# A one-core encoder layer: norm by scaled rows and transposes, three weight blocks before the second half of the tokens, a half-width triangular inverse, another order at the end, and new stage times

## The chip, the cores and the metric

The kernel runs on one core of one Trainium2 chip. The metric is the device time of one execution in microseconds; before the change the median of three runs is 1065.43 us (1065.08 to 1065.56). A profile comes from one execution more, and times within it are counted from its first instruction.

## The reference

One layer of an encoder, 512 tokens of 1024 channels in float32: a norm, one wide projection `w_in`, two token-mixing branches, a gated merge through `w_out`, a second norm, a SwiGLU feed-forward, and a last norm.

```python
h = rmsnorm(x, mix_norm[l])
p = h @ w_in[l]
rx, ry, qkv, z, ba, gates = jnp.split(p, SPLIT_IDX, axis=-1)
y_rnn = rglru_branch(rx, ry, ...) @ w_rnn_proj[l]        # conv, gates by 128x128 blocks, scans both ways
y_dn = deltanet_branch(qkv, z, ba, ...) @ w_dn_proj[l]   # 8 heads, both ways, a triangular solve per chunk
g_rnn, g_dn = jnp.split(jax.nn.sigmoid(gates), 2, axis=-1)
x = x + (g_rnn * y_rnn + g_dn * y_dn) @ w_out[l]
h = rmsnorm(x, ffn_norm[l])
gt, up = jnp.split(h @ w_gate_up[l], 2, axis=-1)
x = x + (jax.nn.silu(gt) * up) @ w_down[l]
return rmsnorm(x, final_norm)                            # rmsnorm: y = x * rsqrt(mean(x*x)+EPS) * g
```

## The kernel before

**Number format.** Most products are made of three single-pass matmuls: an operand is split into a rounded part (`hi`, on ACT) and the rest (`lo`, on DVE), and hi·hi, hi·lo and lo·hi are added up in PSUM (`mm3`). A column block of `w_in` is 1024x128 numbers, 512 KB; it is fetched by SP into one of three `wraw` buffers, split by ACT and DVE, and multiplied with `hh` and `hl`, the split of the normed and transposed tokens. A block takes 24 matmuls of 512 tokens, or 48 of 256: the first blocks are worked in two halves of the tokens (`in_proj`), since half of `hh` is there earlier.

**First norm.** Tokens lie on partitions, 128 to a tile (`xs`, four tiles). `rms_rstd` sums the squares of a tile (ACT for tiles 0 and 2, DVE for 1 and 3), takes the root on ACT and the reciprocal on DVE. `norm_scale` makes a diagonal matrix `dg` of it, and `norm_transpose` multiplies the raw tile with `dg` on PE, in full float32, which transposes and scales at once; ACT and DVE then write `hh` and `hl` with the gain, 128 channels by 256 tokens at a time. Beside it a small block `C_BA` of 32 columns (split into 64) gives the decays and betas.

**Branches.** `rg_front` makes a column block, a convolution and four gate products; groups of three blocks share their activation tables. For the delta branch heads go in four groups of two: `dn_front` (projections), `dn_mats` (masked decays `dts` and the matrices `na`), `dn_inverse` (inverse of 16 unit-triangular 128x128 matrices: 32x32 blocks by back substitution on DVE, merged on PE), `dn_state` (the recurrence over four chunks), `dn_out`. In `dn_mats` POOL masks the decay differences and ACT takes four exponentials of them. The back substitution runs over rows l = 30 to 1, and each step multiplies an l by (31-l) rectangle and subtracts it. POOL also makes the `kd` factors of the state.

**Feed-forward and end.** Gate/up and down projections use a seven-product scheme on DVE-made sums. The end takes four token tiles one after the other: last matmuls, add to the residual, sum of squares, root, and two pieces written out, the low half by ACT (`xg`) and the high half by DVE in two parts of 256. The last tile is number 1, and its last 256 columns come from a bank of their own.

**Order.** Nothing is issued as written. `Rec` records each operation with an estimated cost and a due time, `plan.t`; `spend` starts a new stage, and `TIMES` holds one number per stage that replaces the stage's base time. `Plan.order` runs a list scheduler over the five engines with these due times, the pools' buffers and the semaphore lags, and the program is issued in the order that it finds. Each engine then works its own list strictly in that order. Since every operation passes through one helper, all have line L377 in the profile before (L379 in the changed kernel); tiles tell them apart.

## Time and profile before

| | before |
|---|---|
| median of 3 runs | 1065.43 us |
| the profiled execution | 1066.06 us, span 1064.3 us |
| PE busy | 1046.5 us, 6767 records |
| DVE busy | 886.2 us |
| ACT busy | 676.8 us |
| POOL busy | 41.3 us |
| moved from and to HBM | 121.7 MB, 114 GB/s |

The span runs from the first to the last instruction; the profiled execution's own time is 1.76 us more. PE is the matmul engine, DVE, ACT and POOL the other three that compute, SP issues most transfers. In a row of the timeline stand the start, the length, the engine, the operation, what it writes and reads, and in brackets how long the engine had been idle and what ended that. A float32 matmul that isn't split runs in two passes, so that the 32 diagonal products stand as 64 records; a matmul's recorded length has a tail that overlaps the next one, so that the pace is read from start to start.

### The profile page before, as it was taken

The numbers are of one execution on the slowest core, as the hardware profiler recorded it, in microseconds if no ns is written. First come the engines' busy times: TensorE is split into PE (matmuls) and PEld (weight loads), VectorE is DVE, ScalarE is ACT, GpSimd is POOL, SyncE is SP. The second block draws the span as 40 slices with busy tenths as digits, with TensorE's granted clock in tenths as the row PEclk, the third lists the DMA queues.
The fourth block names the chain that finished last, engine by engine and source line by source line (L and its number), as shares of the span: only waits on it lengthen the run. The fifth ranks groups of instructions, "written<-read, shape, count | busy, mean of one in ns | idle before, by whom it ended". The sixth has DMA issues, their size and how long they took to land.

```text
span 1064.3 us, 17717 instructions
## 1 busy us (share of the span) xinstructions
PE 1046.5 (98%) x6767; PEld 911.6 (86%) x6767; DVE 886.2 (83%) x1598; ACT 676.8 (64%) x1240; POOL 41.3 (4%) x93
## 2 busy tenths in 40 slices
PE   7999999999999999999999999999999999999997
PEld 6988888788888887988888898779999999998885
DVE  6668999869985896699489658469999989889997
ACT  6899989888448866467654644347444544545664
POOL 2100000002001200102000000000000000000000
PEclk9999999999999999999999999999999999999999
DMA  7422323233322342123213324454577433325643
GB/s 201 133 85 81 99 82 102 85 109 106 103 85 70 90 114 80 41 79 80 55 24 106 90 76 137 140 177 150 179 230 241 135 102 102 114 92 186 214 135 106
DMA packets 174389, 122.83 MB, mean 115 GB/s; under 512 B 5952, under 2 KB 160720, under 8 KB 174304
## 3 DMA queue, kind: packets, MB, share of 16 engines
q1 hardware_dynamic: 172832, 118.41, 37.6%
q10 hardware_dynamic: 1184, 3.15, 0.8%
q8 instruction: 53, 0.87, 0.4%
q14 instruction: 32, 0.26, 0.1%
q0 software_dynamic: 288, 0.13, 0.1%
HBM read 113.78 MB, written 7.90 MB: 114 GB/s over the span
## 4 chain that ended last, share of the span: by engine, by line
PE 84%; ACT 8%; DVE 3%; DMA 2%; issue 1%; SPq 0%; ACTq 0%; DVEq 0%
PE mm L377 50%; PE ax L377 22%; PE st L377 13%; ACT t L377 5%; DVE t L377 2%; ACT L377 2%; DMA wraw<-in_w_gate_up_dram 1%; ACT whi L377 1%; DMA wraw<-in_w_out_dram 1%; DVE wlo L377 1%; DVE na L377 0%; ACT na L377 0%; DMA t<-in_x_dram 0%; DMA t<-gcr 0%; ACT ax L377 0%
## 5 line engine op out<-in xcount | busy, mean ns | idle before, releaser
L377 DVE TENSOR_TENSOR t<-t,t 128x512 fp32r<-128x512 f32 (+18 forms) x466 | 245.2, 543 | 20.0 <-ACT t L377 12.3
L377 PE MATMUL mm<-hl,whi 128*128 128x512 f32 (+2 forms) x704 | 242.4, 356 | 0.0
L377 PE MATMUL mm<-hh,whi 128*128 128x512 f32 (+2 forms) x704 | 241.9, 355 | 0.0
L377 ACT CAST whi<-wraw 128x1024 fp32r<-128x1024 f32 (+3 forms) x142 | 133.5, 941 | 147.9 <-PE mm L377 76.4
L377 DVE TENSOR_TENSOR wlo<-wraw,whi 128x1024 fp32r<-128x1024 f32 (+3 forms) x141 | 153.4, 1088 | 65.4 <-PE mm L377 29.9
L377 PE MATMUL mm<-hh,wlo 128*128 128x512 f32 (+1 forms) x688 | 156.1, 357 | 0.0
L377 PEld LDWEIGHTS mm<-hl,whi 128*128 128x128 f32 (+1 forms) x704 | 132.5, 188 | 17.7 <-DVE hl L377 0.9
L377 PEld LDWEIGHTS mm<-hh,whi 128*128 128x128 f32 (+1 forms) x704 | 132.5, 188 | 16.8 <-issue 0.2
L377 PE MATMUL ax<-t,t 32*32 32x32 f32 (+3 forms) x1062 | 139.6, 286 | 0.3
L377 PEld LDWEIGHTS mm<-hh,wlo 128*128 128x128 f32 x688 | 115.5, 189 | 16.7
L377 PEld LDWEIGHTS ax<-t,t 128*128 128x128 f32 (+1 forms) x1062 | 108.7, 159 | 17.4 <-ACT t L377 3.2
L377 ACT CAST t<-t 128x512 fp32r<-128x512 f32 (+2 forms) x128 | 81.7, 652 | 56.1 <-DVE t L377 51.0
L377 PE MATMUL mm<-t,t 128*128 128x256 f32 (+1 forms) x468 | 91.2, 336 | 1.7 <-DVE t L377 1.3
L377 ACT ACT_TABLE_LOAD x67 | 86.0, 1283 | 4.9 <-PEq L1574 1.7
L377 DVE SCALAR_TENSOR_TENSOR t<-mm,par,t 128x511 f32<-128x511 f32 (+1 forms) x108 | 80.0, 742 | 6.8 <-ACT t L377 6.0
L377 PEld LDWEIGHTS mm<-t,t 128*128 128x128 f32 x468 | 72.7, 190 | 11.4 <-DVE t L377 2.0
L377 PE MATMUL mm<-t,whi 128*128 128x512 f32 x320 | 82.2, 395 | 0.2 <-ACT whi L377 0.2
L377 PEld LDWEIGHTS mm<-t,whi 128*128 128x128 f32 x320 | 59.6, 188 | 12.7 <-ACT whi L377 0.6
L377 ACT ACTIVATE t<-t 128x128 f32<-128x128 f32 (+4 forms) x84 | 46.2, 559 | 20.2 <-DVE t L377 17.9
L377 ACT CAST t<-wraw 128x1024 fp32r<-128x1024 f32 (+1 forms) x48 | 41.9, 872 | 25.4 <-DMA wraw<-in_w_gate_up_dram 15.6
L377 DVE TENSOR_TENSOR t<-wraw,t 128x1024 fp32r<-128x1024 f32 (+1 forms) x48 | 48.1, 1002 | 1.5 <-ACT t L377 1.4
L377 PE MATMUL mm<-t,wlo 128*128 128x512 f32 x160 | 42.3, 393 | 0.0
(208 smaller groups left out, 1648.3 us busy)
## 6 DMA issues: line engine op xcount, KB each, us to landing
wraw<-in_w_in_dram SPq DMA_DIRECT2D x72, 512.0 KB, 3.8
wraw<-in_w_gate_up_dram SPq DMA_DIRECT2D x44, 512.0 KB, 4.3
wraw<-in_w_rnn_proj_dram SPq DMA_DIRECT2D x16, 384.0 KB, 3.5
bg<-in_w_down_dram SPq DMA_DIRECT2D x11, 512.0 KB, 4.2
sums<-bg SPq DMA_DIRECT2D x11, 512.0 KB, 4.6
wraw<-sums SPq DMA_DIRECT2D x11, 512.0 KB, 4.8
wraw<-in_w_down_dram SPq DMA_DIRECT2D x22, 256.0 KB, 3.0
wraw<-in_w_down_dram SPq DMA_DIRECT2D x11, 512.0 KB, 3.6
```

The source lines that it names most:

```text
L377: self.plan.add(e, lambda: real(*a, **kw), outs, ins, cost, tail, table)
```

## The change

The core of the diff; the other lines of `TIMES`, and code that only moved (`parts_of`, `weights_k`), are left out.

```diff
 TIMES = [
-    -119957, -57429, -53220, -81357, -34218, -3669, -11726, -34954, -94128, -14279, -5671, -1137, -4316, -201, -3421,
+    -153745, -118892, -151742, -141630, -118601, -110624, -115268, -33958, -18020, -66486, -73432, -37443, -49540,
...
-                    cost = 33 if cols == 32 else 81 if cols == 64 else n * 4 / 2.4 + 10
+                    cost = 22 if cols == 32 else 76 if cols == 64 else n * 4 / 2.4 + 10
...
+                if op == "activation":
+                    cost = max(cost, 200)
...
+    def rms_rstd(src, halves):
+        sa, rst, rin = (small([P, 1], t, 4) for t in ("ssq", "rst", "rin"))
+        n = 512 if halves else D
+        A.activation(four(shape=(P, D))[:, 0:n], src[:, 0:n], AF.Square, accum_out=sa)
+        bias = eps_t
+        if halves:
+            bias = small([P, 1], "ssh", 4)
+            V.scalar_tensor_tensor(two(), src[:, n:D], 1.0, src[:, n:D], ALU.mult, ALU.mult, accum_out=bias)
+            V.tensor_scalar(bias, bias, 1.0 / D, EPS, ALU.mult, ALU.add)
+        act(rst, sa, AF.Sqrt, scale=1.0 / D, bias=bias)
         V.reciprocal(rin, rst)
         return rin
...
+        for i, src in enumerate(srcs):
+            t = four(shape=(P, D))
+            V.tensor_scalar(t, src, rms_rstd(src, i == 0), None, ALU.mult)
+            sc.append(t)
...
-                    T.matmul(pt[...], srcs[i][:, kt * P:(kt + 1) * P], dgs[i], start=True, stop=True)
+                    turn(pt[...], sc[i][:, kt * P:(kt + 1) * P])
...
+    idle = axb()
+    plan.extra = (len(plan.ops) - 2,)
+    for i in range(10):
+        T.matmul(idle[:, 0:P], ones, ones, start=True, stop=True)
+    plan.extra = ()
...
+    norm_transpose(xs[0:2], gain, hh, hl, 0)
+    spend()
+    for c in range(2, NT):
+        load_x(c)
+    norm_transpose(xs[2:4], gain, hh, hl, 2)
+    spend()
...
-        hi, lo = weights(win[:, :, col:col + P], KD, P, admit)
+        hi, lo = (weights_k if len(first_tiles) < 3 else weights)(win[:, :, col:col + P], KD, P, admit)
...
-        mm3(..., KD, 2 if len(first_tiles) < 4 else 1)
+        mm3(..., KD, 2 if len(first_tiles) < 3 else 1)
...
-        plan.t = now - 40
+        plan.t = now - (40 if b > 2 else 12)
...
+                G.affine_select(out=ds, in_=dv, pattern=[[0, NT], [1 - 2 * d, P]], compare_op=ALU.is_gt, fill=0.0, base=0,
+                                channel_multiplier=2 * d - 1)
...
-        B, X = four(shape=(P, 32, 32)), four(shape=(P, 32, 32))
+        B, X = four(shape=(P, 32, 32)), two(shape=(P, 32, 16))
...
         for l in range(30, 0, -1):
-            n = 31 - l
+            j0 = (l + 1) // 2
+            n = 16 - j0
...
+            write_low(i, xg, rin0)
...
-            A.activation(two()[:, 0:256], xv[:, 256:512], AF.Square, accum_out=ssf[:, i, 2:3])
-        write(i, xg, finish(i))
+            added = (len(plan.ops) - 1,)
+            V.scalar_tensor_tensor(two()[:, 0:256], xv[:, 256:512], 1.0, xv[:, 256:512], ALU.mult, ALU.mult, accum_out=ssf[:, i, 2:3])
+            rin1 = finish(i)
+            write_high(0, rin0, added)
+            write(i, xg, rin1)
```

In words: the first norm scales whole tiles on DVE and transposes them on PE in one pass; the sum of squares of tiles 0 and 2 is made in halves on ACT and DVE, that of tiles 1 and 3 on ACT alone. Ten float32 matmuls of a matrix of ones are issued on PE before the first transposes. The loads of tiles 2 and 3 come in a stage of their own. The first three column blocks have buffers of the larger pool and work in halves of the tokens (four did so before). In the inverse the even and odd columns of each 32x32 block lie on different partitions, so that a step's rectangle is about half as wide; it needs matrices with an empty diagonal, which a second mask on POOL gives (16 operations more). At the end the low half of tile 0 is written as soon as its norm is there, its high half after the last addition to tile 1, and the last sum of squares is made on DVE. Two costs of the planner and all stage times are new.

The first place is ACT's list at the start; `t_91` to `t_94` are the token tiles, `wraw_182` the first column block, `whi_141` the small block, and `ax_113` to `ax_116` hold the transposed first half. Before:

```order
L377 ACTIVATE t_102,ssq_101<-t_91 128x1024
L377 ACTIVATE rst_103<-ssq_101,eps_t_89 128x1
L377 ACTIVATE rst_108<-ssq_106,eps_t_89 128x1
L377 ACTIVATE t_116,ssq_115<-t_93 128x1024
L377 ACTIVATE rst_117<-ssq_115,eps_t_89 128x1
L377 CAST whi_135<-wraw_134 128x8x32
L377 ACTIVATE hh_98<-ax_110,gain_97 128x256 x2
L377 ACTIVATE rst_122<-ssq_120,eps_t_89 128x1
L377 ACTIVATE hh_98<-ax_111,gain_97 128x256 x2
L377 ACTIVATE hh_98<-ax_112,gain_97 128x256 x2
```

And now (rows that wait for different things are put apart only by their tiles):

```order
L379 ACTIVATE t_105,ssq_102<-t_91 128x512
L379 ACTIVATE rst_103<-ssq_102,ssh_106 128x1
L379 ACTIVATE t_112,ssq_109<-t_92 128x1024
L379 CAST whi_141<-wraw_140 128x8x32
L379 ACTIVATE rst_110<-ssq_109,eps_t_89 128x1
L379 CAST t_183<-wraw_182 128x1024
L379 ACTIVATE hh_99<-ax_113,gain_97 128x256 x2
L379 ACTIVATE hh_99<-ax_114,gain_97 128x256 x2
L379 ACTIVATE hh_99<-ax_115,gain_97 128x256 x2
L379 ACTIVATE t_121,ssq_118<-t_93 128x512
L379 ACTIVATE hh_99<-ax_116,gain_97 128x256 x2
```

The cast of the first column block has moved ahead of the first piece of `hh`, and the squares of tiles 2 and 3 behind most of the first half.

The second place is DVE's list around the end of the kernel: `st_1701` (now `st_1711`) is the bank of the last 256 columns, `rin_1911` (now `rin_1921`) the norm of tile 0, `rin_1917` (now `rin_1927`) that of tile 1. Before:

```order
L377 RECIPROCAL rin_1911<-rst_1910 128x1
L377 TENSOR_TENSOR t_1913<-na_1120,t_1898 128x512
L377 SCALAR_TENSOR_TENSOR na_1120<-na_1120,rin_1911,t_1898 128x256 x2
L377 TENSOR_TENSOR na_1120<-st_1701,na_1120 128x256
L377 TENSOR_SCALAR rst_1916<-ssf_1696 128x1
L377 SCALAR_TENSOR_TENSOR rst_1916<-ssf_1696,rst_1916 128x1
L377 RECIPROCAL rin_1917<-rst_1916 128x1
L377 SCALAR_TENSOR_TENSOR na_1120<-na_1120,rin_1917,t_1898 128x256 x2
```

And now:

```order
L379 RECIPROCAL rin_1921<-rst_1920 128x1
L379 TENSOR_TENSOR t_1923<-na_1130,t_1908 128x512
L379 TENSOR_TENSOR na_1130<-st_1711,na_1130 128x256
L379 TENSOR_SCALAR rst_1926<-ssf_1706 128x1
L379 SCALAR_TENSOR_TENSOR t_1925,ssf_1706<-na_1130 128x256
L379 SCALAR_TENSOR_TENSOR rst_1926<-ssf_1706,rst_1926 128x1
L379 SCALAR_TENSOR_TENSOR na_1130<-na_1130,rin_1921,t_1908 128x256 x2
L379 RECIPROCAL rin_1927<-rst_1926 128x1
L379 SCALAR_TENSOR_TENSOR na_1130<-na_1130,rin_1927,t_1908 128x256 x2
```

The two scalings of tile 0 went from ahead of the last addition to just ahead of the last reciprocal, and a sum of squares has come to DVE.

The third place is PE's list where `w_out` begins; `mm_991` is the last gate block before, `mm_1124` the last piece of the delta branch's projection now, and the others are products of `w_out`. Before:

```order
L377 MATMUL mm_991<-hh_98,whi_989 128x512
L377 MATMUL mm_991<-hl_99,whi_989 128x512
L377 MATMUL mm_991<-hh_98,wlo_990 128x512 x8
L377 MATMUL mm_1170<-t_1164,t_1113 128x512
L377 MATMUL mm_1176<-t_1156,t_1083 128x512
L377 MATMUL mm_1176<-t_1155,t_1083 128x512
L377 MATMUL mm_1176<-t_1158,t_1089 128x512
```

And now:

```order
L379 MATMUL mm_1186<-t_1165,t_1093 128x512
L379 MATMUL mm_1124<-t_1080,whi_1126 128x512 x2
L379 MATMUL mm_1124<-t_1081,whi_1126 128x512 x2
L379 MATMUL mm_1124<-t_1080,wlo_1127 128x512
L379 MATMUL mm_1124<-t_1081,wlo_1127 128x512
L379 MATMUL mm_1186<-t_1168,t_1099 128x512
L379 MATMUL mm_1186<-t_1169,t_1099 128x512
```

Before, the last gate block was worked just ahead of the remaining `w_out` products, and 20 of them stood between it and the first that needs the last merged channels; now all gate blocks stand earlier, the last projection piece stands there, and 15 products stand between it and the first that needs them. From the feed-forward on the lists are nearly the same in both.

## The prediction

> **What bounds the kernel now.** I read the page's totals first, then PE's waits, then the chain that ended last.

> ```profile
> span 1064.3 us, 17717 instructions
> PE 1046.5 (98%) x6767; PEld 911.6 (86%) x6767; DVE 886.2 (83%) x1598; ACT 676.8 (64%) x1240; POOL 41.3 (4%) x93
> PE 84%; ACT 8%; DVE 3%; DMA 2%; issue 1%; SPq 0%; ACTq 0%; DVEq 0%
> ```

> PE is busy for 1046.5 of 1064.3 us and holds 84% of the chain that ended last; 17.8 us are left to win without taking work from it. The view of PE's waits says where most of them lie.

> ```profile
> PE ax L377 <- DVE dg L377: 3.9, 2, 3.5
> PE ax L377 <- DVE loc L377: 2.9, 1, 2.9
> PE mm L377 <- DVE t L377: 1.3, 2, 1.0
> PE ax L377 <- ACT t L377: 0.5, 1, 0.5
> PE mm L377 <- ACT t L377: 0.3, 1, 0.3
> PE ax L377 <- ACT na L377: 0.3, 1, 0.3
> PE mm L377 <- ACT whi L377: 0.2, 1, 0.2
> ```

> The first number is the sum, the second the count. 6.8 us are the start (`dg`, `loc`), 2.6 us the five other kinds together, and the rest is mostly the tail, since the last matmuls end by 1056.38 of 1064.3 (row below). So three places can move the time: PE's work and waits at the start, the 2.6 us in between, and the tail. Work of DVE, ACT or POOL elsewhere is worth nothing unless PE comes to wait for it.

> **The change part by part: the start.** The mark is the end of the norm, the small block and two column blocks, which are the same products before and now; the third column block begins there. Before, PE reaches it at 33.87.

> ```profile
> 6.66 1.65 PE L377 MATMUL ax<-dg,t 128*128 128x128 f32 x6 [3.55 <-DVE dg L377]
> 8.65 4.21 PE L377 MATMUL ax<-dg,t 128*128 128x128 f32 x18 [0.35 <-DVE dg L377]
> 13.30 1.33 PE L377 MATMUL ax<-dg,t 128*128 128x128 f32 x10
> 24.65 0.46 PE L377 MATMUL ax<-ident,t 64*128 64x64 f32 x4
> 32.91 1.12 PE L377 MATMUL mm<-hh,wlo 128*128 128x256 f32 x8
> 33.87 0.28 PE L377 MATMUL mm<-hh,whi 128*128 128x256 f32 x1
> L377 PE MATMUL ax<-dg,t 128*128 128x128 f32 x64 | 11.1, 336 | 3.9 <-DVE dg L377 3.9
> ```

> The 32 products with `dg` stand as 64 passes. Eighteen of them take 4.21 us at 8.65, ten take 1.33 at 13.30: about 0.22 and 0.11 us from start to start, so PE runs at half pace until about 13.3. Eight matmuls of 256 tokens go from 32.91 to 33.87: 0.12 each. The change makes 32 passes of the 64. At full pace 32 x 0.11 = 3.6 us of PE go, and the 0.35 us of waiting may go too: **-4 is the best end** of this term.

> The ten matmuls of ones stand as 20 passes, 20 x 0.22 = 4.4 us at half pace. They are ready early (`loc` comes at 2.9) and end at about 7.4, while the first transposes can come at about 6.8, so they cost at most 0.6 us of a stretch in which PE then waits for `hl` anyway.

> The rest is a race of ACT and DVE, which make `hh` and `hl`. Their prices:

> ```profile
> 4.61 1.06 ACT L377 ACTIVATE t<-t 128x1024 f32<-128x1024 f32 x1 [1.37 <-DMA t<-in_x_dram]
> 6.12 0.16 DVE L377 RECIPROCAL rin<-rst 128x1 f32<-128x1 f32 x1 [2.80 <-ACT rst L377]
> L377 DVE TENSOR_SCALAR t<-na,rin 128x1024 f32<-128x1024 f32 x4 | 3.0, 746 | 0.0
> L377 DVE SCALAR_TENSOR_TENSOR t<-na 128x512 f32<-128x512 f32 x4 | 2.7, 684 | 0.0
> 10.96 0.83 ACT L377 ACTIVATE hh<-ax,gain 128x256 fp32r<-128x256 f32 x2
> 13.63 1.04 ACT L377 CAST whi<-wraw 128x1024 fp32r<-128x1024 f32 x1
> 13.77 0.88 DVE L377 SCALAR_TENSOR_TENSOR hl<-ax,gain,hh 128x256 fp32r<-128x256 f32 x2 [0.15 <-ACT hh L377]
> 14.96 1.22 DVE L377 TENSOR_TENSOR wlo<-wraw,whi 128x1024 fp32r<-128x1024 f32 x1
> ```

> Tile 0 is there at 4.61. Half its squares take ACT about half of 1.06 and a read-out; DVE's half takes 0.68. With root and reciprocal the scale is ready at about 6.0 (6.28 before), but the whole tile must be scaled, 0.75 against 0.29 us for `dg`: first transpose at about 6.8 (6.66 before). Nothing is won here.

> SP now asks for the first column block ahead of tiles 2 and 3, which come later by its 512 KB; at 283 GB/s (the row of the stretch 10 to 15, in rival B) that is 1.85 us, and their squares aren't due on ACT before the first half's `hh`. Then DVE goes on, with 0.88 per pair of `hl`, 1.22 per `lo` of a block. My working by its list: the first half's pairs and the first block's `lo` end at 15.7 (`hl` trails `hh`, and ACT has the block's cast of 1.04 ahead of `hh`); the two scalings of tiles 2 and 3 at 19.3 (0.75 each, behind ACT's squares of both tiles and the roots); two `lo` of 1.22 at 21.75; the first two pairs of the second half at 23.5; a gate's `lo` of 0.69 and a third block's of 1.22 at 25.4; the last two pairs at 27.2. PE meanwhile does the first half of the blocks. From 21.5 it has left 66 products at 0.12, 8 transposes at 0.11, the four small ones of 0.46, 9.2 us together; with about 0.6 of waits for the late pairs it is done at 31.2 (an estimate from these rows). **33.87 to 31.2 is -2.7 us.** The other end is +1.2: one `lo` of 1.22 that stands ahead of the last pairs and isn't covered.

> [...]

> **The middle.** The column block that is no longer split takes 24 matmuls of 512 in place of 48 of 256: 24 x 0.23 = 5.5 against 48 x 0.12 = 5.8 (0.23 is 4.54 us over 20 in the first row below, without the last one's tail), hence at most -0.3, within the bounds below. The one wait that I can follow stands where `w_out` begins.

> ```profile
> 700.31 4.70 PE L377 MATMUL mm<-t,t 128*128 128x512 f32 x20
> 702.69 2.15 DVE L377 TENSOR_TENSOR t<-t,t 128x512 f32<-128x512 f32 x3 [0.89 <-ACT t L377]
> 704.87 0.62 ACT L377 CAST t<-t 128x512 fp32r<-128x512 f32 x1 [2.21 <-DVE t L377]
> 705.54 0.50 PE L377 MATMUL ax<-whi,t 128*128 128x512 f32 x1 [0.53 <-ACT t L377]
> ```

> PE runs 20 matmuls in about 4.54 us and still waits 0.53 for the last merged channels: three DVE operations of 0.72, then a cast of 0.62. Now the last piece of the delta projection ends just ahead of its merge, with 15 matmuls behind it, 15 x 0.23 = 3.4 us, while the merge needs about 0.7 + 0.7 + 0.62 and three hops of some 0.15, 2.5 us: that wait goes (-0.5). Of the 0.3, 0.3 and 0.2 about half go by the new order (-0.3 with rounding to what a wait costs at its edges); the 1.3 stays, since its two places lie at about 797 and 819, in the feed-forward, whose order is the same. **-0.8**, between -2.6 (every wait gone) and +2.6 (as much again).

> The inverse is cheaper on DVE and dearer on POOL.

> ```profile
> L377 DVE TENSOR_TENSOR t<-t,t 128x240 f32<-128x240 f32 x16 | 6.5, 406 | 0.4
> L377 DVE TENSOR_TENSOR t<-t,t 128x30 f32<-128x30 f32 x16 | 3.2, 199 | 0.2
> L377 POOL TENSOR_SCALAR_AFFINE_SELECT t<-t 128x512 f32<-128x512 f32 x16 | 12.9, 818 | 221.3 <-DMA t<-gcr 139.4 <-DVE t L377 81.2 <-DVE nq L377 0.6
> ```

> From 240 to 30 elements an operation falls by 0.207 us, 1 ns per element. The rectangles l(31-l) have 165 elements on average, so halving them saves about 0.083 us in each of 240 operations (30 steps, two each, four groups): 20 us of DVE. It buys nothing by itself, because PE waits only 0.3 us for anything of this part (`na`). Without that cover it would be 5 us a group. The 16 further masks are 16 x 0.82 = 13 us of POOL, which idles for most of the span: 0, with the other side in rival D.

> **The end.** Here every step is on the path.

> ```profile
> 1055.14 1.24 PE L377 MATMUL st<-t,t 128*128 128x256 f32 x9
> 1056.38 0.61 ACT L377 ACTIVATE t<-na 128x512 f32<-128x512 f32 x1
> 1056.59 0.67 DVE L377 TENSOR_TENSOR t<-na,t 128x512 f32<-128x512 f32 x1
> 1057.18 0.87 DVE L377 SCALAR_TENSOR_TENSOR na<-na,rin,t 128x256 f32<-128x256 f32 x2
> 1057.97 0.42 DVE L377 TENSOR_TENSOR na<-st,na 128x256 f32<-128x256 f32 x1
> 1058.53 0.42 ACT L377 ACTIVATE t<-na 128x256 f32<-128x256 f32 x1 [0.43 <-DVE rst L377]
> 1059.40 0.16 DVE L377 RECIPROCAL rin<-rst 128x1 f32<-128x1 f32 x1 [0.68 <-ACT rst L377]
> ```

> The last addition comes 0.8 earlier, at 1057.18, as the two scalings (0.87) no longer stand ahead. The sum of squares on DVE takes no more than ACT's 0.42 and its read-out, so the root could come 0.8 earlier, at about 1058.3. But the two scalings now stand ahead of the last reciprocal: from 1058.3 they hold DVE to about 1059.2, where the reciprocal was at 1059.40. **-0.2**, between -0.5 (they fit into the time of the root) and +0.4 (one scaling more than fits).

> **The sum**: -2.7 - 0.8 - 0.2 = -3.7. The profiled execution took 1066.06 us (1.76 more than its span), so it would take 1062.4; it lies 0.63 above the median of 1065.43, and the forecast for the median is 1061.7.

> **The rivals.**
> [...]
> B. ACT's cast of the first column block stands ahead of `hh`, and more `lo` ahead of `hl`. If those weights land with or behind the tokens, `hh` waits, and the start gives nothing: +2.7, 1064.4, and as much as 1065.6 with the 1.2 of one `lo`. For: the transfers share one rate, 283 GB/s in the stretch from 10 to 15 (the column ahead of it is their share, 1.20, and 1.00 the clock).

> ```profile
> 10.00:15.00 5.00, 5.00 (x32) 5.00 (x32) 4.46 (x13) 4.16 (x11) 0.00 (x0) 1.00 1.20 283
> ```

> Against: the block is asked for ahead of tiles 2 and 3, so by its 1.85 us it lands about when `hh` starts.
> C. All waits of the middle go (-2.6) and the start gives its 4: -6.8, 1058.6. For: DVE has 20 us more room. Against: the feed-forward's 1.3 lie where nothing changes.
> D. **Slower**: the second mask. Each of the 16 stands between the differences and an exponential, so 16 x (0.82 + 0.15 for a hop) = 15.5 us enter the chain that gives `na`. If half isn't covered, +7.8 - 3.7 = +4.1, 1069.5. It decides from 1.5 us of PE waiting per group on, where it eats 3.7 and 2.1 more. For: POOL's masks wait for DVE (81.2), so they lie in a chain. Against: PE waits 0.3 for `na`, other blocks are at hand, and DVE's steps become shorter by 5 us a group, more than 4 x 0.97 = 3.9.
> That the ones or the end do nothing is within the terms.

> **How the numbers follow.** A measurement of this kernel can tell about 0.2%, 2.13 us, from no change: faster is below 1063.3, slower above 1067.6. Forecast 0.55 (1059.5 to 1063.3), A 0.08, B 0.16, C 0.10, D 0.11. Faster: forecast, C and most of A, 0.70; same: B and the rest of A, 0.19; slower: D, 0.11. The range goes from 1058.3, which takes in C and both best ends, to 1066.0, which takes in B with its 1.2; what lies above is D and a little of the middle's +2.6.

> **What would show it.** In the changed profile: the third column block's first product at about 31.2; the wait for `dg` gone, with a first transpose at about 6.8; transposes 0.11 apart from the first on (A wrong) or 0.22 (A right); a cast ahead of `hh` with a wait for `wraw` (B); no wait of PE for ACT where `w_out` begins; DVE about 20 us less busy and POOL 13 more, with PE's waits for `na` still below 1 us (D wrong); the last reciprocal 2.8 us behind the last matmul, in place of 3.0. The forecast is wrong if PE's waits between 34 and 1040 grow beyond 3 us, or if the start wins less than 1.

## The result and the profile after

| | before | changed |
|---|---|---|
| median, 22 runs each, side by side | 1066.50 us | 1064.87 us |
| ratio | | 0.9988, 95% interval 0.9977 to 0.9998 |
| the profiled execution | 1066.06 us, span 1064.3 | 1068.03 us, span 1066.3 |

By the ratio the change gains 1.3 us, 0.12%, where 3.7 us, 0.35%, was forecast. The time lies in the range, but the gain is smaller than a measurement of this kernel tells clearly. One number needs care: executions of one kernel differ by some us, and the profiled one of the changed kernel took 3.2 us more than its median; what follows uses what came again in a second profile (first experiment).

The totals and PE's waits of the changed kernel:

```profile
span 1066.3 us, 17661 instructions
PE 1045.2 (98%) x6731; PEld 908.7 (85%) x6731; DVE 867.6 (81%) x1606; ACT 675.7 (63%) x1244; POOL 53.0 (5%) x109
```

```profile
PE ax L379 <- DVE t L379: 4.2, 4, 2.1
...
PE ax L379 <- issue: 1.8, 1, 1.8
...
PE ax L379 <- DVE na L379: 0.7, 1, 0.7
```

DVE has 18.6 us less to do and POOL 11.7 more, nearly as worked out. But there are new waits: 2.1 us for DVE in one piece, 1.8 us of "issue" (PE waits for nothing that the profile shows) and 0.7 for `na`. Behind the start, PE's waits of 0.15 us and more sum to 7.3 us now, to 2.7 before.

**The start** won a little more than forecast. PE's timeline of the changed kernel:

```profile
3.20 3.98 PE L379 MATMUL ax<-ones 128*128 128x128 f32 x20
7.01 0.55 PE L379 MATMUL ax<-ident,t 128*128 128x128 f32 x3
8.47 1.20 PE L379 MATMUL ax<-ident,t 128*128 128x128 f32 x9 [0.91 <-DVE t L379]
...
28.21 0.46 PE L379 MATMUL ax<-ident,t 64*128 64x64 f32 x4 [0.56 <-ACT t L379]
28.60 0.39 PE L379 MATMUL mm<-hl,t 128*128 128x256 f32 x1
...
29.53 1.24 PE L379 MATMUL mm<-hh,t 128*128 128x256 f32 x9
30.61 0.28 PE L379 MATMUL mm<-hl,t 128*128 128x256 f32 x1
```

Nine transposes take 1.20 us, 0.11 apart: full pace from 8.47, where the diagonal products ran at half pace until 13.3. The product at 28.60, behind the four small transposes, is still one of the second block: in PE's list 15 of that block's 48 products stand behind these transposes, seven up to 29.53 and the first eight of the nine there. The ninth is the first product of the third block. It starts at 30.49 (0.12 ahead of the next row), before at 33.87: -3.4 us. The expectations below date the third block by the product behind the small transposes, 1.9 us early; the text gives its real start, and the differences between runs of the changed order are the same either way.

**The end** won more as well. From the end of the last addition on, in the changed kernel:

```profile
1059.59 0.42 DVE L379 TENSOR_TENSOR na<-st,na 128x256 f32<-128x256 f32 x1
...
1060.05 0.43 DVE L379 SCALAR_TENSOR_TENSOR t<-na 128x256 f32<-128x256 f32 x1
...
1060.47 0.87 DVE L379 SCALAR_TENSOR_TENSOR na<-na,rin,t 128x256 f32<-128x256 f32 x2
...
1060.93 0.29 ACT L379 ACTIVATE rst<-ssf,rst 128x1 f32<-128x1 f32 x1 [0.42 <-DVE rst L379]
1061.26 0.16 DVE L379 RECIPROCAL rin<-rst 128x1 f32<-128x1 f32 x1
```

The last matmuls end at 1058.80, and the last reciprocal starts 2.46 later; before it was 1056.38 to 1059.40, 3.02. The two scalings (0.87) fit into the root's time: the root ends at 1061.22, and the reciprocal follows 0.04 later, as it did before (1059.36 to 1059.40). So -0.56, of which 0.4 are left at the span's end.

**The middle** gave it back: in this execution the last matmul ends 2.4 us later than before, in spite of the 3.4 won at the start, so the middle lost 5.8. The first place is the second inverse (heads 2 and 3). DVE and PE in the changed kernel, two answers of the timeline:

```profile
373.11 0.88 DVE L379 SCALAR_TENSOR_TENSOR na<-ax,dns,t 128x256 f32<-128x256 f32 x2 [1.51 <-POOL t L379]
...
380.32 1.66 DVE L379 SCALAR_TENSOR_TENSOR na<-ax,dns,t 128x256 f32<-128x256 f32 x4
...
416.25 1.22 DVE L379 TENSOR_TENSOR wlo<-wraw,whi 128x1024 fp32r<-128x1024 f32 x1
417.39 0.70 DVE L379 STREAM_TRANSPOSE t<-t 128x512 f32<-128x512 f32 x1
```

```profile
418.15 0.75 PE L379 MATMUL ax<-t,na 32*32 32x32 f32 x64 [2.09 <-DVE t L379]
```

And the matching rows of before, DVE and PE:

```profile
362.75 1.66 DVE L377 SCALAR_TENSOR_TENSOR na<-ax,dns,t 128x256 f32<-128x256 f32 x4 [1.01 <-PE ax L377]
364.92 1.78 DVE L377 STREAM_TRANSPOSE t<-na 32x256 f32<-32x256 f32 x4
```

```profile
412.93 0.75 PE L377 MATMUL ax<-t,na 32*32 32x32 f32 x64
```

Before, `na` is done at 364.4 and the merge begins at 412.9, 48.5 us later, without a wait. Now the way from `na` to the merge is shorter, 382.0 to 418.1, 36.1 us, but `na` comes 17.6 us later, where DVE waits for POOL on the way: POOL runs the last four of its eight masks of these heads between 368.3 and 376.2, where all had been done by 247.9. PE waits 2.09 at the merge. Which part of this way the masks cost is read from the run without them, below.

The second place is the third inverse, PE's timeline of the changed kernel:

```profile
507.87 0.75 PE L379 MATMUL ax<-t,na 32*32 32x32 f32 x64
...
510.14 0.92 PE L379 MATMUL ax<-t,t 32*32 32x32 f32 x84
512.85 0.28 PE L379 MATMUL ax<-t,t 32*32 32x32 f32 x12 [1.79 <-issue]
```

In the midst of 96 small matmuls PE stops for 1.79 us, though all operands are there. And a wait can cost more than itself: PE's granted clock behind the wait at 418 (the column after the counts):

```profile
416.00:418.00 2.00, 0.05 (x1) 1.00 0.00 0
418.00:420.00 2.00, 1.85 (x68) 0.83 0.59 166
420.00:422.00 2.00, 2.00 (x56) 0.50 0.36 104
422.00:424.00 2.00, 2.00 (x36) 0.81 0.00 0
```

For 3.4 us PE had half its clock. The lost clock is 2 x 0.17 + 2 x 0.50 + 2 x 0.19 = 1.7 us.

### The profile page after: what moved, and what is told of

Read it like the earlier page. It is cut to its first block, busy times and chain, and to the rows that moved or that the text cites. A ratio compares the mean times of both kernels' runs of the same rounds, so it can differ in the third digit from the quotient of the medians.

```text
span 1066.3 us, 17661 instructions
## 1 busy us (share of the span) xinstructions
PE 1045.2 (98%) x6731; PEld 908.7 (85%) x6731; DVE 867.6 (81%) x1606; ACT 675.7 (63%) x1244; POOL 53.0 (5%) x109
## 4 chain that ended last, share of the span: by engine, by line
PE 71%; DVE 14%; ACT 8%; issue 4%; DMA 3%; POOL 0%; SPq 0%; DVEq 0%; ACTq 0%; POOLq 0%
PE mm L379 43%; PE ax L379 18%; PE st L379 10%; DVE t L379 9%; ACT t L379 5%; DVE wlo L379 3%; ACT L379 1%; DVE na L379 1%; ACT whi L379 1%; ACT ax L379 1%; DMA wraw<-sums 1%; DMA wraw<-in_w_in_dram 1%; DMA wraw<-in_w_gate_up_dram 1%; DMA bg<-in_w_down_dram 1%; DVE hl L379 0%
## 5 line engine op out<-in xcount | busy, mean ns | idle before, releaser
L379 DVE TENSOR_TENSOR t<-t,t 128x512 fp32r<-128x512 f32 (+23 forms) x466 | 226.7, 501 | 14.8 <-ACT t L379 6.3
L379 PE MATMUL mm<-hh,whi 128*128 128x512 f32 (+2 forms) x648 | 229.4, 363 | 0.4 <-ACT hh L379 0.4
L379 PE MATMUL mm<-hl,whi 128*128 128x512 f32 (+2 forms) x648 | 228.9, 362 | 0.8 <-DVE hl L379 0.8
L379 ACT CAST whi<-wraw 128x1024 fp32r<-128x1024 f32 (+3 forms) x139 | 130.1, 937 | 155.2 <-PE mm L379 87.8
L379 DVE TENSOR_TENSOR wlo<-wraw,whi 128x1024 fp32r<-128x1024 f32 (+3 forms) x138 | 150.4, 1092 | 75.1 <-PE mm L379 27.4
L379 PE MATMUL mm<-hh,wlo 128*128 128x512 f32 (+1 forms) x632 | 146.8, 364 | 0.0
L379 PEld LDWEIGHTS mm<-hl,whi 128*128 128x128 f32 (+1 forms) x648 | 121.8, 188 | 18.5 <-DVE hl L379 1.2
L379 PEld LDWEIGHTS mm<-hh,whi 128*128 128x128 f32 (+1 forms) x648 | 121.7, 188 | 17.8 <-ACT hh L379 0.7
L379 PEld LDWEIGHTS mm<-hh,wlo 128*128 128x128 f32 x632 | 109.1, 190 | 17.4
L379 PEld LDWEIGHTS mm<-t,t 128*128 128x128 f32 x468 | 72.4, 190 | 11.1 <-DVE t L379 2.5
L379 DVE TENSOR_TENSOR t<-wraw,t 128x1024 fp32r<-128x1024 f32 (+1 forms) x51 | 51.7, 1016 | 6.1 <-ACT t L379 5.9
```

The costliest lines, as they stand in the source:

```text
L379: self.plan.add(e, lambda: real(*a, **kw), outs, ins, cost, tail, table)
```

## The experiments

The theory after this reading: the start's gain is real, and the middle loses it at named places by the new order and by the inverse's later inputs and masks, with one stop whose cause is open. Rivals: PE's gain at the start is absorbed in any case, or the middle is chance.

**The same kernel again.** 

> The changed kernel once more, for what repeats in it. If the waits behind the start are set by the order (order theory), the 2.1 us for DVE's t at about 418 us comes again, and the 0.7 us for na near 248 too; the 1.8 us of 'issue' at 513 us should be chance and be gone or elsewhere. The third column block begins at 28.6 us again. If instead the middle is chance in all its parts (rival), the waits between 34 and 1040 us sum to another value, 3 us or less. Time 0.1% under the kernel before.

Ratio 0.9996 (0.9981 to 1.0011). The wait at 418 came again (1.79), that for `na` too (0.66), and the third block began at 29.92. The stop of "issue" was no chance: 1.93 us at the same place, between the 84th and the 85th of the 96 matmuls. The slow clock did not come again at its place: behind 418 it stayed at 1.00, and fell to 0.50 behind the stop instead. Over all runs with the changed order there were eight gaps of 1.8 to 2.1 us at these two places, and the clock fell behind these two alone. So what repeats is order and place.

**The start alone.** The old inverse, end and planner costs; stage times of the new norm and two blocks, then the old ones:

```diff
-TIMES = [ ... new ... ]
+TIMES = new[:6] + old[3:]
```

> The new first norm, ones and first column blocks alone: old inverse with one mask, old end, old planner costs, and the old stage times behind the first two column blocks. Order theory (the start wins 5 us, the new order and inverse behind it lose it): the third column block begins near 29 us and the time falls by 4 to 5 us, 0.4 to 0.5%. Absorption theory (whatever PE wins at the start it waits for later, since DVE, ACT and the weights come no earlier): PE's waits between 34 and 700 us grow by 3 us or more and the time falls by at most 1.5 us.

Neither: 0.36% slower (1.0036, 1.0024 to 1.0048). The third block began at 29.8, then PE met one long wait, and by 100 us a lead of some 5 us over the kernel before had become a lag of 4 (an estimate from the products done by then); behind it the kernel ran much like before. PE's row, and ACT's groups between 50 and 84 us:

```profile
80.91 0.80 PE L379 MATMUL mm<-hh,whi 128*128 128x512 f32 x1 [7.21 <-ACT whi L379]
```

```profile
L379 ACT ACT_TABLE_LOAD x8 | 10.3, 1283 | 0.1
```

In that stretch ACT had five table loads before and has eight now, because with old times the first gates' exponentials and sigmoids fall between each other; the cast that PE waits for stands behind them. So in this kernel a start that runs 4 us earlier needs stage times that fit it: here the old ones cost more than the start won.

**All the new code, old times from the fourth block on.** 

> All the new code, with the old stage times from the fourth column block on. If the new stage times are what loses behind the start: 4 to 6 us under the kernel before (0.4 to 0.55%), PE's waits between 34 and 1040 us at 3 us or less. If the inverse with its second mask loses (mask theory): PE waits for na or for the inverse as in the changed kernel, 3 us and more, and the time is 0 to 2 us under the kernel before.

1.98% slower (1.0198, 1.0177 to 1.0219): 14 waits of 0.56 to 4.4 us behind 34 us, spread over the kernel. Both expectations fall. The old times don't fit the new code, and this run can't say whether the masks are to blame. The next ones hold the order fixed instead: the planner's list is kept, and single operations are taken out of it, exchanged or added.

**Without the ones, replanned.** 

> The changed kernel without the ten matmuls of ones. If they are what brings the clock up: the first transposes are 0.21 us apart instead of 0.11, half pace lasts until 10 to 13 us, and the third column block begins 0.5 to 2 us later. If the norm is held by ACT and DVE alone (rival), the start of that block moves by less than 0.3 us. What becomes of it at the end is within 2 us either way.

0.28% slower (1.0028, 1.0016 to 1.0040); nine transposes took 2.18 us, and the third block began at 31.24, 0.75 later. But leaving ten matmuls out changed the planner's whole list, with waits of 1.7 us at 172 and 1.5 at 423, so that the run mixes two things. With the order held it reads otherwise.

**Without the ones, order held.**

```diff
     for i in range(10):
         T.matmul(idle[:, 0:P], ones, ones, start=True, stop=True)
+        plan.ops[-1] = plan.ops[-1][:1] + (lambda: None,) + plan.ops[-1][2:]
```

> Order held, the ten matmuls of ones left out. Start: transposes 0.21 us apart as half pace lasts longer, the third column block begins 1 to 2 us later than 28.6 if the ones carry the start, under 0.5 us if ACT and DVE do. Fetch theory: 40 records fewer, so the stop at 508 goes and one of about 1.6 us comes in the last inverse, at about 598 us; collision theory: it stays at 508.

0.9981 (0.9970 to 0.9991). PE's rows:

```profile
595.32 0.85 PE L379 MATMUL ax<-t,t 32*32 32x32 f32 x76
597.86 0.33 PE L379 MATMUL ax<-t,t 32*32 32x32 f32 x20 [1.69 <-issue]
```

The nine transposes again took 2.18, yet the third block moved by 0.35 us only, to 30.84: ACT and DVE carry the start, not the clock, and the 3.4 us are the norm's and the first blocks' new order. And the stop left 512 and came at 598, as the fetch theory had it; a collision with transfers at 512 would have left it there.

**The stop: 28 pairs more.** The ten ones became 24 of 53 columns, order held. 

> Order of the changed kernel held; the ten matmuls of 128 columns of ones become 24 of 53, the same work in 28 more passes, so that PE's instructions behind them lie 56 records further on. Fetch theory (the stop of 1.8 to 1.9 us in the third inverse's 32x32 matmuls is PE's instructions being fetched in blocks of 256, with the block's edge inside both runs of small matmuls): the stop at about 508 to 513 us is gone and no other of over 0.5 us comes in the 32x32 runs, since the edge now lies outside; with the slower clock behind it the time falls by 2 to 3 us against the changed kernel, 0.2 to 0.3%. If the stop has another cause (rival: a collision with transfers at that point), it stays where it is and the time stays the same.

0.11% slower than before (1.0011, 1.0001 to 1.0022). PE's rows:

```profile
3.17 10.48 PE L527 MATMUL ax<-ones 128*128 128x53 f32 x48
```

```profile
513.33 0.69 PE L379 MATMUL ax<-t,t 32*32 32x32 f32 x56
515.89 0.54 PE L379 MATMUL ax<-t,t 32*32 32x32 f32 x40 [1.87 <-issue]
```

A miss in two ways. A pass of 53 columns took as long as one of 128 at half pace (10.48 / 48 = 0.22 us; the eighteen of 128 before are 0.22 apart), so the ones held the norm up until 13.5. And the stop did not vanish. But it moved, from behind 84 matmuls to behind 56: 28 pairs earlier in the run for 28 pairs more in front. In this run, both profiles of the changed kernel and three others 6081 of PE's records (in the changed kernel 6049 matmuls and weight loads and 32 more of its queue) start ahead of the matmul that stops; in the other runs with a stop of "issue" it is another count (3265, 4546, 5057, 7361, 7362). Divided by 256 each leaves 193 or 194. The changed kernel's page names the transfers:

```profile
q8 instruction: 53, 0.87, 0.3%
```

0.87 MB in 53 packets are 16 KB each, and in the plain stretches one starts about every 256 of PE's matmuls and loads. The two runs without the ones, some 40 records fewer, have 52 packets, the one with 332 more (next run) has 54: one packet for each block of 256.

The packets' times in the traces settle the cause. In the changed kernel the block's packet starts at 510.36 and takes 1.16 us; PE comes to the edge at 510.87 (the last record ahead of it) and goes on at 512.85. In 14 traces with some 730 edges, the packet of a block started at least 2.5 us ahead of PE at every edge that PE crossed without a stop. At the 11 stops it had started 0.1 to 0.9 us ahead (stops of 1.2 to 2.1 us) or 2.1 to 2.2 (the two stops of 0.5 and 0.6), and PE went on 2.3 to 2.9 us behind the packet's start. PE eats a block in some 1.4 us of small matmuls (an estimate: 64 of them, with their loads, from 507.87 to 508.55) and so gets to an edge before its block is there.

**The kernel before, its instructions moved.** 

> The kernel before, order held, with 83 matmuls of 32x32 in the idle 3.5 us of PE ahead of its first diagonal products: no other work, and PE's instructions lie 166 records further on, so that an edge comes into the third inverse's first run of small matmuls, as in the changed kernel. Fetch theory: a stop of 'issue' of 1.5 to 2.1 us appears in that inverse (at about 512 us) and the kernel is 1.5 to 3 us slower, 0.15 to 0.3%, with the same order: the kernel before had none by the chance of its layout. Rival (the stop belongs to the changed order): no stop, same time within 0.5 us.

0.32% slower (1.0032, 1.0020 to 1.0044), mostly for another reason than expected. PE's rows:

```profile
3.07 9.06 PE L488 MATMUL ax<-ones 32*32 32x32 f32 x166
12.78 1.65 PE L377 MATMUL ax<-dg,t 128*128 128x128 f32 x6 [0.65 <-DVE dg L377]
```

```profile
421.20 0.77 PE L377 MATMUL ax<-t,t 32*32 32x32 f32 x67
422.50 0.38 PE L377 MATMUL ax<-t,t 32*32 32x32 f32 x29 [0.53 <-issue]
```

A small float32 matmul was two passes of 0.055 us at half pace (83 matmuls, 166 records, 9.06 us), so the norm began 6.1 us late, and the instructions moved by 332 records, not 166. A stop did come, in the second inverse and of 0.53 us only. So the old order stops too when its layout falls so, and the rival, that the stop belongs to the changed order, is refuted; a stop of full size was not shown in it. The shift of 332 had also put the edge into another inverse than planned. The run shows one thing more: the 6.1 us at the start were 3.3 at the last matmul (1059.66 against 1056.38). The waits of 0.34, 0.53, 0.98 and 0.35 that PE had at 668, 705, 797 and 820 are gone, so a late PE gets 2.2 us back there.

**The inverse: one exchange on DVE.**

```diff
         todo = plan.order()
+        at = todo.index(last_turn[1])
+        ahead = max(k for k in range(at) if plan.ops[todo[k]][0] == "DVE")
+        todo.insert(ahead, todo.pop(at))
```

> Order held but for one exchange on DVE: in the second inverse (heads 2 and 3) the last transpose of the inverse goes ahead of the 1.22 us split of a column block that stood just before it. If DVE's list is what PE waits for at 418 us: the wait of 1.8 to 2.1 us becomes 0.6 to 0.9, and the lag behind it 1.2 us less. If something else holds the merge (ACT's copies, or the masks), the wait changes by less than 0.3.

0.9970 (0.9959 to 0.9981). DVE's rows and PE's:

```profile
416.20 0.71 DVE L379 STREAM_TRANSPOSE t<-t 128x512 f32<-128x512 f32 x1
416.83 1.18 DVE L379 TENSOR_TENSOR wlo<-wraw,whi 128x1024 fp32r<-128x1024 f32 x1
```

```profile
416.97 0.75 PE L379 MATMUL ax<-t,na 32*32 32x32 f32 x64 [0.44 <-DVE t L379]
```

The wait fell to 0.44, by 1.35 and 1.65 against the two profiles and a little below what was expected, and in PE's view no wait for the split appears that now comes later. DVE's list is what PE waited for.

**Without the second masks.** The products read the first mask's half twice, order held. 

> Order held, the 16 second masks left out; the products take the first mask's tile for both halves, so the inverse is made of matrices with a diagonal and the result isn't the reference's. Mask theory: DVE's wait of 1.5 us for POOL at 373 us goes, PE's wait for the inverse at 418 falls by 1 us or more and its wait for na at 248 (0.7) goes; with them 1 to 2.5 us. If masks aren't in the chain (rival): both waits stay within 0.3 us.

0.9971 (0.9958 to 0.9985). DVE's rows and PE's:

```profile
370.98 0.86 DVE L903 SCALAR_TENSOR_TENSOR na<-ax,dns,t 128x256 f32<-128x256 f32 x2
373.90 1.22 DVE L379 TENSOR_TENSOR wlo<-wraw,whi 128x1024 fp32r<-128x1024 f32 x1 [2.05 <-ACT whi L379]
...
388.77 0.23 DVE L379 TENSOR_TENSOR t<-t,t 128x30 f32<-128x30 f32 x1
```

```profile
416.31 0.75 PE L379 MATMUL ax<-t,na 32*32 32x32 f32 x64 [0.80 <-DVE t L379]
```

The wait at 418 is 0.80 (from 2.09 and 1.79) and that for `na` at 248 is gone: the second masks cost 1.7 to 2 us of PE's waits. But at 418 they do it in another way than thought. DVE no longer waits for POOL at 373, yet it then waits 2.05 for ACT, and the next operation is only 0.54 us earlier than in the changed kernel (373.90 against 374.44), a lead that DVE had before that wait. The rest comes later: while one of POOL's masks runs, an operation of DVE can take some 0.4 us longer. In the changed kernel, DVE and POOL:

```profile
389.31 0.65 DVE L379 TENSOR_TENSOR t<-t,t 128x30 f32<-128x30 f32 x1
```

```profile
388.76 1.14 POOL L379 TENSOR_SCALAR_AFFINE_SELECT t<-t 128x512 f32<-128x512 f32 x1 [7.84 <-ACT t L379]
```

The same operation takes 0.23 above. Between 388 and 407 three second masks of the next heads fall into this inverse; without them DVE's lead grows there from 0.54 to 1.83 us, three times 0.43, and the merge's wait falls by 1.0 to 1.3.

**The end, put back.** 

> The changed kernel with the old end (both scalings of tile 0 ahead of the last addition, the last sum of squares on ACT). From the end of the last matmul to the last reciprocal 3.0 us as before, where the changed kernel takes 2.5; so 0.5 to 0.6 us longer behind the last matmul, and nothing elsewhere.

```profile
1054.33 1.24 PE L379 MATMUL st<-t,t 128*128 128x256 f32 x9
```

```profile
1058.59 0.16 DVE L379 RECIPROCAL rin<-rst 128x1 f32<-128x1 f32 x1 [0.69 <-ACT rst L379]
```

From 1055.57 to 1058.59 are 3.02 us, as before: the new end is worth 0.56. This is one execution.

**Repairs.** The exchange on DVE, and PE's instructions moved so that no edge falls badly. The first try counted a small matmul as one pass. 

> Order of the changed kernel held, with the exchange on DVE in the second inverse, and four of the ten ones replaced by 40 matmuls of 32x32: 32 pairs of instructions more, so that no edge of 256 lies inside a first run of 64 small matmuls whose second run is unbroken. Fetch theory: no stop of 'issue' at 508 to 513 and none at 597; PE's wait at 418 at 0.4 as in the run with the exchange alone; start as before (third column block at about 28.3). Together 4 to 5 us under the kernel before, 0.4 to 0.5%. If the stop comes back at another place (rival), 2 to 3 us under it.

0.9979 (0.9967 to 0.9991): the third inverse ran through, but the first one got a stop, and the start lost 1.7 us to 80 passes.

```profile
310.79 0.39 PE L379 MATMUL mm<-hl,whi 128*128 128x512 f32 x1 [1.23 <-issue]
```

The second try took four of the ones and 22 small matmuls:

```diff
+        if i < 6:
+            plan.ops[-1] = plan.ops[-1][:1] + ((lambda m: lambda: [nc.tensor.matmul(idle[0:32, 128:160], ones[0:32, 0:32], ones[0:32, 0:32], start=True, stop=True, tile_position=(0, 0)) for _ in range(m)])(4 if i < 4 else 3),) + plan.ops[-1][2:]
```

> The repair again, with the shift counted as the last runs showed it (a float32 matmul is two passes, each a pair of instructions): four of the ten ones and 22 matmuls of 32x32 in place of ten ones, 52 pairs against 20 in the same 4 us, so 64 records further on, and the exchange on DVE in the second inverse. Fetch theory: the third inverse's first run of small matmuls then begins some 10 records behind an edge, the last one's some 70, and no stop of 'issue' of over 0.5 us is left; the third column block begins at 28.3 to 28.9; PE's wait at 418 is 0.4 to 0.5; 4 to 5 us under the kernel before, 0.35 to 0.5%. If a stop comes up elsewhere (rival), 2 to 3 us.

```profile
417.12 0.75 PE L379 MATMUL ax<-t,na 32*32 32x32 f32 x64 [0.58 <-DVE t L379]
...
507.74 1.02 PE L379 MATMUL ax<-t,t 32*32 32x32 f32 x96
...
594.36 1.02 PE L379 MATMUL ax<-t,t 32*32 32x32 f32 x96
```

0.9949 (0.9933 to 0.9964), 1059.96 against 1065.48 us: 5.5 us under the kernel before, the best of all, with no stop of "issue" at all; the exchange alone had 0.9970. The third block began at 31.02 (-2.85) and the last matmul ended at 1050.74 (-5.64), so the middle takes 2.8 us less than before. The two repairs give back what the change had lost.

## Why the prediction was wrong

- **What bounds the kernel**: right. PE's waits decided, and 18.6 us less of DVE's work bought nothing by itself.
- **The start, -2.7**: right in mechanism and near in size, -3.4 (and -3.95 the second time), within the bound of -4. The working by DVE's list was late by 2.05 us: the last pairs of `hl` ended at 25.15, not 27.2, since the first half was done at 14.66 in place of 15.7 and the scalings at 17.70 in place of 19.3. Only 0.7 of this reached the third block (30.49 in place of 31.2). Rival A, half pace until about 13 at +1.0, fell: behind the ones the nine transposes ran at full pace, in 1.20 us. No run shows its +1.0: without the ones they took 2.18, and the third block began 0.35 later. The clock column of 1.00 in rival B's row doesn't speak against the half pace: the trace's clock record begins only with the full clock, at 13.41 before and 6.33 now, and ahead of that the rows' distances decide. Rival B fell: `hh` started at 9.56, behind a cast that waited 1.32 for its weights, and the start won all the same.
- **The middle, -0.8**: this is the step that failed; it measured +5.8 and +4.1. Its named wait did go: at 705 PE no longer waits. The hop, put at some 0.15, is 0.03 us from DVE to ACT and 0.05 from ACT to PE there (before, 704.84 to 704.87 and 705.49 to 705.54), and 0.13 from ACT to POOL (changed, 388.63 to 388.76). But "It buys nothing by itself, because PE waits only 0.3 us for anything of this part" was read as a price of 0 for the whole inverse. That small wait was the result of masks made 100 us ahead; the changed order makes half of those of heads 2 and 3 just in time and ends DVE's work on the inverse late, and then a wait of 1.8 to 2.1 us stands at 418 and one of 0.7 at 248. Rival D named the second masks, at +7.8, and they measured 1.7 to 2; its way, a mask in the chain to `na`, holds for the wait at 248 and not for the larger part, where POOL's masks make DVE's operations longer. No row before had a stop of "issue"; no term and no rival had instruction fetching, which cost 1.8 to 1.9 us. The prediction's own sign of being wrong came: PE's waits between 34 and 1040 us grew by 4.7 and 4.2 us, beyond 3.
- **The end, -0.2**: right in mechanism, -0.56 in size, a little beyond the bound of -0.5: the scalings fitted into the time of the root.
- **The sum**: -3.4 (start), -0.4 (end), +4.7 (waits of the middle, the stop among them), -0.6 (two more blocks behind the mark are unsplit, at the prediction's 0.3 each) and +1.7 (the clock) give +2.0, as the first profile has it. With -3.95 and +4.2 the second comes to +0.95 where its span is 0.2 shorter than before, so that 1.1 us of it stay unexplained. The clock's lapse came in both profiles, once at each place; without it the sums are +0.3 and -0.75, where the two comparisons measured -1.3 and -0.4. That the time lies in the range says little for the middle: the range reached up to 1066.0, half a us below the 1066.50 that the kernel before had beside it.

What stays open: why a block's packet starts 4.0 us ahead of PE at the edge before in one place (last inverse of the changed kernel, no stop) and 2.3 behind it in another (third inverse); why the clock fell behind two of the eight gaps; and by what POOL's masks make DVE's operations longer.

## What to carry to other kernels

A wait that is small in the profile tells what the present order hides, not what the part costs; when an edit lengthens a chain and the order is made anew, price the chain as if its inputs came just in time. Where a change is to be judged to 0.2%, test single terms with the order held fixed, since replanning after a small edit moved this kernel by more than the edits did (0.3% to 2%). And when PE stops in a dense run of small matmuls with nothing to wait for, count its instructions: moving them by some dozens can be worth as much as the change.
